# Placing the high and low parts of streamed weights: one place in a 256-byte line for all, or two for each product

## The chip, the cores and the metric

The kernel runs on one core of a Trainium2 chip. The metric is the device time of one launch in microseconds; the median of three runs of the kernel before is 1408.38 us (1407.89 to 1414.13). All rows shown come from one profiled execution.

## What is computed

The reference is one layer of a hybrid decoder on 256 tokens of width 2048, all in float32: a root-mean-square norm, an input projection, sliding-window attention beside a state-space mixer (whose inputs first go through a causal convolution along the tokens), an output projection, and then a feed-forward network with a convolution, a gate and a down projection. Cut to the lines that matter here:

```python
proj = xn @ w_in                                  # 2048 -> q, k, v, z, conv channels, dt
xbc = jax.nn.silu(_causal_dwconv(xbc, ssd_conv_w, ssd_conv_b))
...
h = h + jnp.concatenate([attn, y], axis=-1) @ w_out
...
u = _causal_dwconv(hn @ w_up, ffn_conv_w, ffn_conv_b)       # 2048 -> 2 * 5632
gate, val = u[..., :D_FF], u[..., D_FF:]
h = h + (jax.nn.silu(gate) * val) @ w_down                  # 5632 -> 2048
return _rmsnorm(h, norm_final)
```

## The kernel before, in words

Weights stream from HBM in blocks of 1 MB (tile `raw`, 128 partitions x 2048 floats). Each half block of 1024 floats per partition is split into a high part, rounded to the matmul's float32r type by ScalarE (`hi`, line 80), and a low part, the rest, subtracted by VectorE (`lo`, line 81). The activations are split in the same way and stay in memory, the high and the low row of a 128-row tile side by side: `xT` before the mixer, `h2T` before the feed-forward network. A product in this split form is high x high + high x low + low x high.

There are two kinds of product. `gemm_tok` keeps the activations stationary in TensorE's array and streams the weights past them, 512 columns at a time; query, key, value, gate, output and down projections go this way. `gemm_chan` keeps the weights stationary, 128 x 128 at a time, and streams the 256 tokens past them. It is used for two stages:

- The conv stage: 8 products of 512 output channels (two for each of four turns `zi`, with `gemm_tok` products between them). With `wide=False` each weight tile pair costs three matmuls of 256 columns: high weights on high tokens (line 229), high weights on low tokens (line 230), low weights on high tokens (line 231). That is 192 matmuls in a product and 1,536 in the stage.
- The up stage: 22 products of 512 output channels, one after the other (11 turns `c`, two products each). Each weight tile pair costs two matmuls: high weights on high and low tokens together, 512 columns (line 237), and low weights on the high tokens, 256 columns (line 235). That is 64 pairs in a product and 1,408 in the stage.

Every one of these matmuls is preceded by its own weight load (PEld in the profile), which runs beside the matmul before it: beside a 512-column matmul the low weights are loaded, beside a 256-column matmul of the up stage the next high weights.

`hi` and `lo` are rings of four tiles each, every tile beginning at a multiple of `LINE` = 256 bytes. A product's data begin `at` bytes into the tile. All slices used as weights begin a multiple of 512 bytes further on, and the token rows are 1024 bytes apart, so within one stage all weight tiles of a kind have one place modulo 256, and so have all token rows. Before the change the places are: `W_AT` = 0 for high and low weights of the up stage and of all `gemm_tok` products, `C_AT` = 64 for high and low weights of the conv stage; `X_AT` = 0 for `xT` and the other activations, `H_AT` = 32 for `h2T`. The order of the instructions comes from a scheduler that is run when the program is built.

Of the kernel before, what the change touches and what calls it, by code (L numbers as in the profile page):

```python
# [11 lines left out]
F32R = mybir.dt.float32r  # L12
# [7 lines left out]
P = 128  # L20
# [18 lines left out]
HALF = 1024  # L39
LINE = 256  # L40

W_AT, C_AT, X_AT, H_AT = 0, 64, 0, 32

PAR_MIX, PAR_ATT, PAR_SSD, PAR_FFN = 0, 16, 32, 48
PAR_CW, PAR_CB = 64, 192
# [7 lines left out]
def hymba(ctx, tc, x, xt, w_kd, w_in, w_out, w_up, w_down, par, vecs, gfin, con, out):  # L53
# [4 lines left out]
    wp = ctx.enter_context(tc.tile_pool(name="wp", bufs=1))  # L58
# [4 lines left out]
    def acc(tag="acc"):  # L63
        return ps.tile([P, 512], F32, tag=tag, name=tag, bufs=4)
# [9 lines left out]

    def split(raw, o, n, at):
        hi, lo = (
            wp.tile([P, HALF + C_AT // 4], F32R, tag=t, name=t, bufs=4, align_bytes=LINE)[:, at // 4 : at // 4 + n]
            for t in ("hi", "lo")
        )
        A.copy(out=hi, in_=raw[:, o : o + n])  # L80
        V.tensor_tensor(out=lo, in0=raw[:, o : o + n], in1=hi.bitcast(F32), op=ALU.subtract)  # L81
        return hi, lo

    def pieces(src, width, parts, load=None, work=None, at=W_AT):

        n = width // parts
        per = RAWW // n
        raws = [wp.tile([P, RAWW], F32, tag="raw", name="raw", bufs=3) for _ in range(-(-parts // per))]
        part = lambda h: raws[h // per][:, h % per * n : (h % per + 1) * n]
        if load:  # L90
            for h in range(parts):
                load(h)
                SY.dma_start(out=part(h), in_=src[:, h * n : (h + 1) * n])
        else:
            SY.dma_start(out=raws[0][:, :width], in_=src)
        out = []
        for h in range(parts):
            if work:
                work(h)
            out.append(split(part(h), 0, n, at))  # L100
        return out

    def acts(pool, at, **kw):
        return placed(pool, NKT * 2 * S, at, **kw).rearrange("p (k i s) -> p k i s", i=2, s=S)

    xT = acts(cp, X_AT, tag="xT", name="xT")
# [74 lines left out]
    def step(n=1):  # L181
        turn[0] += n
        while side and side[0][0] <= turn[0]:
            heappop(side)[2]()
# [24 lines left out]
                if i < nb - 1 or m < 3:  # L209
                    step()  # L210

    def gemm_chan(blocks, actT, evac, tag="acc", wide=True):

        b = [acc(tag) for _ in range(4)]
        nb = len(blocks)
        for i, src in enumerate(blocks):
            got = pieces(src, 2048, 2, at=W_AT if wide else C_AT)
            last = i == nb - 1
            for ks in [(0, 1, 2, 3)] if last else [(0, 1), (2, 3)]:
                for ct in range(4):  # L220
                    for k in ks:
                        hi, lo = got[k // 2]
                        kt = 4 * i + k
                        o = (k % 2) * 512 + ct * P
                        end = kt == NKT - 1
                        rh = actT[:, kt, 0, :]
                        wh, wl = hi[:, o : o + P], lo[:, o : o + P]
                        if not wide:
                            PE.matmul(out=b[ct][:, :S], lhsT=wh, rhs=rh, start=kt == 0, stop=False)  # L229
                            PE.matmul(out=b[ct][:, :S], lhsT=wh, rhs=actT[:, kt, 1, :], start=False, stop=False)  # L230
                            PE.matmul(out=b[ct][:, :S], lhsT=wl, rhs=rh, start=False, stop=end)  # L231
                            continue
                        for lo_turn in (True, False) if end else (False, True):
                            if lo_turn:
                                PE.matmul(out=b[ct][:, :S], lhsT=wl, rhs=rh, start=False, stop=False)  # L235
                            else:
                                PE.matmul(out=b[ct], lhsT=wh, rhs=actT[:, kt, :, :], start=kt == 0, stop=end)  # L237
                    if last:
                        evac(ct, b[ct])
                    if (ct < 3) if last else (ct % 2):  # L240
                        step()

    def conv(dst, b, rB, wcol, bias, taps, wide):

        u = up.tile([P, S], F32, tag="cu", name="cu", bufs=3)
        if wide:
            A.copy(out=u, in_=b[:, S:])
            V.tensor_tensor(out=u, in0=b[:, :S], in1=u, op=ALU.add)
            V.tensor_tensor(out=u, in0=u, in1=rB, op=ALU.mult)
        else:  # L250
            V.tensor_tensor(out=u, in0=b[:, :S], in1=rB, op=ALU.mult)
        A.activation(out=dst, in_=u, func=AF.Identity, scale=wcol(taps - 1), bias=bias)
        for j in range(1, taps):
            V.scalar_tensor_tensor(  # L254
                out=dst[:, j:], in0=u[:, : S - j], scalar=wcol(taps - 1 - j), in1=dst[:, j:],
                op0=ALU.mult, op1=ALU.add,
            )
# [336 lines left out]
    def decay_load(g):  # L594
        e = sp.tile([P, NT, HPG, P], F32, tag="e", name="e", bufs=2)
        G.dma_start(
            out=e.rearrange("p t h l -> p t (h l)"), in_=acs_d[:, g, :].partition_broadcast(P)
        )
        return e
# [162 lines left out]
    for zi in range(4):  # L762
        es, parts, zt = {}, {}, {}

        def z_load(zi=zi, zt=zt):
            zt[0] = sp.tile([P, NT, 512], F32, tag="zs", name="zs", bufs=1)
            G.dma_start(out=zt[0].rearrange("p t d -> p (t d)"), in_=z_d[zi])

        def decay_loads(zi=zi, es=es):
            for g in (2 * zi, 2 * zi + 1):  # L770
                es[g] = decay_load(g)

        for g in (2 * zi, 2 * zi + 1):
            u = up.tile([P, 4, S], F32, tag="u", name="u", bufs=2)

            def evac_u(ct, b, u=u, g=g, zt=zt):
                cidx = 2 * g + ct if ct < 2 else (16 + g if ct == 2 else 24 + g)
                conv(u[:, ct, :], b, r1B, lambda k: col(PAR_CW + 32 * k, cidx), col(PAR_CB, cidx), 4, False)
                A.activation(out=u[:, ct, :], in_=u[:, ct, :], func=AF.Silu)
                if g % 2 and ct == 3:  # L780
                    A.activation(out=zt[0], in_=zt[0], func=AF.Silu)

            def part(i, g=g, u=u, es=es, parts=parts):
                if i == 0:
                    parts[g] = ssd(g, es, u)
                parts[g][i]()

            gemm_chan([w_in[5 + 3 * zi + g % 2, i] for i in range(4)], xT, evac_u, wide=False)
            if g % 2 == 0:
                later((1 if zi else 11, decay_loads), (4 if zi else 14, z_load))  # L790
            later(*(
                (off, f) for off, f in zip(
                    (5, 7, 11, 13) if g % 2 else (4, 6, 10, 12) if zi else (13, 14, 18, 20),
                    (
                        lambda g=g, es=es: decay(g, es[g]), lambda part=part: part(0),
                        lambda part=part: part(1), lambda part=part: part(2),
                    ),
                )
            ))

        def gates(zi=zi, parts=parts, zt=zt):
            for g in (2 * zi, 2 * zi + 1):
                parts[g][3](zt[0])

        gemm_att(zi)
        later(
            (1, gates), (7, lambda zi=zi, parts=parts: parts[2 * zi][4]()),
            (9, lambda zi=zi, parts=parts: parts[2 * zi + 1][4]()), *(((10, open_hp),) if zi == 3 else ()),
        )
# [30 lines left out]
    for c in range(11):  # L840
        gate = up.tile([P, 4, S], F32, tag="u", name="gate", bufs=2)

        def evac_f(ct, b, val, c=c, gate=gate):
            i = 4 * c + ct
            ci = i + (NFT if val else 0)
            if val:
                dst = fp.tile([P, S], F32, tag="cv", name="cv", bufs=3)
            else:
                dst = gate[:, ct, :]
            conv(dst, b, r2B, lambda k: col(PAR_FW + 88 * k, ci), col(PAR_FB, ci), 3, True)  # L850
            if val:
                G.tensor_tensor(out=gT[:, i, :], in0=gate[:, ct, :], in1=dst, op=ALU.mult)  # L852
            else:
                A.activation(out=dst, in_=dst, func=AF.Silu)

        for val in range(2):
            gemm_chan(
                [w_up[2 * c + val, i] for i in range(4)], h2T, lambda ct, b, val=val: evac_f(ct, b, val),
                tag="aux" if val else "acc",
            )  # L860

    oacc = [[acc("acc" if t == 0 else "aux") for _ in range(4)] for t in range(NT)]
# [162 lines left out]
```

## Time and profile before

| | |
|---|---|
| median of three runs | 1408.38 us |
| the profiled execution | 1410.48 us |
| its span, first to last instruction | 1408.8 us |
| TensorE busy | 1388.7 us, 99% of the span |
| conv stage, first to last of its 8 products | about 270 to 553 us, with other products between |
| up stage | about 670 to 1160 us |
| down projection | about 1160 to 1390 us |

The span is what the trace covers; the 1.7 us between it and the time of that execution lie outside the program's instructions. A matmul's listed duration is longer than the distance from its start to the next start, since matmuls are pipelined; the distances between starts are what adds up.

### The profile page before, as it was taken

Reading aid. Unit: us, or ns where it says so; the run is one execution under the profiler, and the core shown is the slowest. Engines: PE = TensorE matmul, PEld = TensorE weight load, DVE = VectorE, ACT = ScalarE, POOL = GpSimd, SP = SyncE. Lnnn points to the kernel's source line nnn. Section 1 sums busy time; section 2 is a strip of 40 time slices with the busy share of each in tenths; the row PEclk is TensorE's granted clock in tenths of the full one; section 3 lists DMA queues with packets and bytes.
Section 4 is the critical chain, followed back from the end, with each engine's and each line's share of the span. In section 5 each row is a group of like instructions: output and inputs, shape, how many; then the busy total and the mean of one; then the engine's idle time right before and its main releaser. Section 6 shows DMA issues by size and latency. Waiting matters only on the chain.

```text
span 1408.8 us, 20546 instructions
## 1 busy us (share of the span) xinstructions
PE 1388.7 (99%) x7925; PEld 1219.9 (87%) x7925; DVE 969.4 (69%) x1448; ACT 785.4 (56%) x1245; POOL 173.8 (12%) x155
## 2 busy tenths in 40 slices
PE   8999999999999999999999999999999999999997
PEld 8788888997999999888888888888888888888886
DVE  5676876777777767655677768777786766555555
ACT  6666666656756555454555555555554554444444
POOL 0002112022121121200011001110011101000001
PEclk9999999999999999999999999999999999999999
DMA  8754444555656564565655555555555555555552
GB/s 293 271 181 154 176 150 165 184 183 177 235 194 211 193 235 161 207 222 184 221 190 181 178 209 183 198 188 180 202 186 185 195 189 187 201 184 204 183 205 90
DMA packets 44593, 271.76 MB, mean 193 GB/s; under 512 B 5056, under 2 KB 7232, under 8 KB 14672
## 3 DMA queue, kind: packets, MB, share of 16 engines
q1 hardware_dynamic: 40288, 254.69, 50.8%
q0 software_dynamic: 4208, 15.76, 3.6%
q8 instruction: 62, 1.02, 0.3%
q14 instruction: 35, 0.29, 0.1%
HBM read 264.11 MB, written 6.32 MB: 192 GB/s over the span
## 4 chain that ended last, share of the span: by engine, by line
PE 92%; DMA 3%; DVE 2%; ACT 1%; issue 1%; POOL 0%; SPq 0%; DVEq 0%; POOLq 0%; ACTq 0%
PE acc L237 11%; PE aux L237 11%; PE acc L170 11%; PE acc L168 11%; PE acc L169 11%; PE aux L235 6%; PE acc L235 6%; PE acc L231 4%; PE acc L229 4%; PE acc L230 4%; PE aux L169 3%; PE aux L170 3%; PE aux L168 3%; PE aux L464 1%; PE aux L673 1%
## 5 line engine op out<-in xcount | busy, mean ns | idle before, releaser
L81 DVE TENSOR_TENSOR lo<-raw,hi 128x1024 fp32r<-128x1024 f32 (+1 forms) x480 | 588.1, 1232 | 348.0 <-ACT hi L80 345.9
L80 ACT CAST hi<-raw 128x1024 fp32r<-128x1024 f32 (+1 forms) x480 | 492.1, 1034 | 416.8 <-PE aux L170 126.4
L237 PE MATMUL acc<-h2T,hi 128*128 128x512 f32 x704 | 243.4, 391 | 0.0
L237 PE MATMUL aux<-h2T,hi 128*128 128x512 f32 x704 | 243.0, 391 | 0.0
L235 PE MATMUL aux<-h2T,lo 128*128 128x256 f32 x704 | 191.1, 282 | 0.0
L235 PE MATMUL acc<-h2T,lo 128*128 128x256 f32 x704 | 191.0, 282 | 0.0
L237 PEld LDWEIGHTS aux<-h2T,hi 128*128 128x128 f32 x704 | 129.8, 188 | 24.6
L237 PEld LDWEIGHTS acc<-h2T,hi 128*128 128x128 f32 x704 | 129.8, 188 | 24.5
L229 PE MATMUL acc<-xT,hi 128*128 128x256 f32 x512 | 143.2, 282 | 0.0
L230 PE MATMUL acc<-xT,hi 128*128 128x256 f32 x512 | 143.1, 281 | 0.0
L231 PE MATMUL acc<-xT,lo 128*128 128x256 f32 x512 | 141.5, 279 | 0.7 <-DVE lo L81 0.7
L235 PEld LDWEIGHTS acc<-h2T,lo 128*128 128x128 f32 x704 | 132.9, 189 | 3.9
L235 PEld LDWEIGHTS aux<-h2T,lo 128*128 128x128 f32 x704 | 132.9, 189 | 3.8
L168 PE MATMUL acc<-hi,xT 128*128 128x512 f32 (+2 forms) x320 | 115.0, 378 | 5.4 <-ACT hi L80 5.4
L170 PE MATMUL acc<-hi,xT 128*128 128x512 f32 (+2 forms) x320 | 119.1, 374 | 0.0
L169 PE MATMUL acc<-lo,xT 128*128 128x512 f32 (+2 forms) x320 | 118.6, 373 | 0.0
L852 POOL TENSOR_TENSOR gT<-gate,cv 128x256 f32<-128x256 f32 x44 | 61.2, 1392 | 434.5 <-DVE cv L254 424.0
L231 PEld LDWEIGHTS acc<-xT,lo 128*128 128x128 f32 x512 | 96.1, 189 | 1.0 <-DVE lo L81 0.9
L230 PEld LDWEIGHTS acc<-xT,hi 128*128 128x128 f32 x512 | 96.5, 189 | 0.4
L229 PEld LDWEIGHTS acc<-xT,hi 128*128 128x128 f32 x512 | 95.9, 188 | 0.3
L168 PEld LDWEIGHTS acc<-hi,xT 128*128 128x128 f32 x320 | 59.6, 192 | 14.5 <-ACT hi L80 5.4
L170 PEld LDWEIGHTS acc<-hi,xT 128*128 128x128 f32 x320 | 61.2, 191 | 9.5
(221 smaller groups left out, 2288.5 us busy)
## 6 DMA issues: line engine op xcount, KB each, us to landing
raw<-in_w_up SPq DMA_DIRECT2D x88, 1024.0 KB, 4.8
raw<-in_w_in SPq DMA_DIRECT2D x68, 1024.0 KB, 4.9
raw<-in_w_down SPq DMA_DIRECT2D x44, 1024.0 KB, 4.8
raw<-in_w_out SPq DMA_DIRECT2D x32, 1024.0 KB, 4.8
raw<-in_w_kd SPq DMA_DIRECT2D x16, 272.0 KB, 4.8
e<-acs_d POOLq DMA_DIRECT2D x8, 512.0 KB, 6.6
xraw<-in_xt SPq DMA_DIRECT2D x16, 128.0 KB, 4.5
x_r<-in_x SPq DMA_DIRECT2D x2, 1024.0 KB, 7.2
```

The lines of the kernel that those rows point to most:

```text
L80: A.copy(out=hi, in_=raw[:, o : o + n])
L81: V.tensor_tensor(out=lo, in0=raw[:, o : o + n], in1=hi.bitcast(F32), op=ALU.subtract)
L168: PE.matmul(out=o, lhsT=lh, rhs=rh, start=first, stop=False)
L169: PE.matmul(out=o, lhsT=lh, rhs=rl, start=False, stop=False)
L170: PE.matmul(out=o, lhsT=ll, rhs=rh, start=False, stop=last)
L229: PE.matmul(out=b[ct][:, :S], lhsT=wh, rhs=rh, start=kt == 0, stop=False)
L230: PE.matmul(out=b[ct][:, :S], lhsT=wh, rhs=actT[:, kt, 1, :], start=False, stop=False)
L231: PE.matmul(out=b[ct][:, :S], lhsT=wl, rhs=rh, start=False, stop=end)
L235: PE.matmul(out=b[ct][:, :S], lhsT=wl, rhs=rh, start=False, stop=False)
L237: PE.matmul(out=b[ct], lhsT=wh, rhs=actT[:, kt, :, :], start=kt == 0, stop=end)
L464: PE.matmul(out=b[:, i * nk : (i + 1) * nk], lhsT=qs[:, jj, g0 + i, n * P : (n + 1) * P], rhs=ks[:, jj, part, 0:nk], start=part == 0, stop ...
L852: G.tensor_tensor(out=gT[:, i, :], in0=gate[:, ct, :], in1=dst, op=ALU.mult)
```

## The change

`split` takes two places instead of one, the first for `hi` and the second for `lo`. `gemm_chan` gets them from its caller: each of the 8 conv products has its own pair (`CONV_AT`) and each of the 22 up products has its own (`UP_AT`). The first sixteen up pairs have the high part at 0, 16, 32, ... 240 bytes and the low part at those sixteen values in another order; the last six are written out. The seventeenth, (0, 0), is the place before the change. `W_AT` becomes (0, 0), so all `gemm_tok` products keep their place. The tiles grow from 4160 to 4352 bytes; since each begins at a multiple of 256, they stood 4352 bytes apart already, and nothing else in memory moves. On each of the five engines the instructions and their order are the same as before.

```diff
-W_AT, C_AT, X_AT, H_AT = 0, 64, 0, 32
+
+W_AT, X_AT, H_AT = (0, 0), 0, 32
+CONV_AT = ((64, 0), (64, 192), (64, 32), (64, 96), (32, 64), (96, 64), (48, 80), (80, 48))
+UP_AT = tuple((16 * i, 16 * ((7 * i + 4) % 16)) for i in range(16)) + (
+    (0, 0), (0, 32), (32, 0), (96, 32), (32, 96), (0, 96)
+)
...
     def split(raw, o, n, at):
         hi, lo = (
-            wp.tile([P, HALF + C_AT // 4], F32R, tag=t, name=t, bufs=4, align_bytes=LINE)[:, at // 4 : at // 4 + n]
-            for t in ("hi", "lo")
+            wp.tile([P, HALF + LINE // 4], F32R, tag=t, name=t, bufs=4, align_bytes=LINE)[:, a // 4 : a // 4 + n]
+            for t, a in zip(("hi", "lo"), at)
         )
...
-    def gemm_chan(blocks, actT, evac, tag="acc", wide=True):
+    def gemm_chan(blocks, actT, evac, at, tag="acc", wide=True):
...
-            got = pieces(src, 2048, 2, at=W_AT if wide else C_AT)
+            got = pieces(src, 2048, 2, at=at)
...
-            gemm_chan([w_in[5 + 3 * zi + g % 2, i] for i in range(4)], xT, evac_u, wide=False)
+            gemm_chan([w_in[5 + 3 * zi + g % 2, i] for i in range(4)], xT, evac_u, CONV_AT[g], wide=False)
...
-                tag="aux" if val else "acc",
+                UP_AT[2 * c + val], tag="aux" if val else "acc",
```

## Rows read from the trace of the kernel before

**Rows 1.** The page: span, busy time, and the chain that ended last by engine.
```profile
span 1408.8 us, 20546 instructions
...
PE 1388.7 (99%) x7925; PEld 1219.9 (87%) x7925; DVE 969.4 (69%) x1448; ACT 785.4 (56%) x1245; POOL 173.8 (12%) x155
...
PE 92%; DMA 3%; DVE 2%; ACT 1%; issue 1%; POOL 0%; SPq 0%; DVEq 0%; POOLq 0%; ACTq 0%
```

**Rows 2.** The waits of TensorE over the whole span: total us, times, longest.
```profile
PE acc L168 <- ACT hi L80: 5.4, 1, 5.4
PE acc L168 <- DVE cu L251: 1.4, 1, 1.4
...
PE acc L231 <- DVE lo L81: 0.7, 1, 0.7
```

**Rows 3.** Windows: second up product, the twenty after it; last columns clock, DMA share, GB/s.
```profile
693.40:715.60 22.20, 22.20 (x129) 19.64 (x128) 15.70 (x26) 12.83 (x21) 0.00 (x0) 1.00 0.53 189
715.60:1160.15 444.55, 444.55 (x2562) 392.91 (x2560) 330.88 (x486) 246.58 (x365) 56.47 (x40) 1.00 0.54 190
```

**Rows 4.** Timeline of TensorE, up stage: start, duration, instruction; 44 pairs between first and last.
```profile
716.31 0.39 PE L237 MATMUL acc<-h2T,hi 128*128 128x512 f32 x1
716.54 0.28 PE L235 MATMUL acc<-h2T,lo 128*128 128x256 f32 x1
716.66 0.39 PE L237 MATMUL acc<-h2T,hi 128*128 128x512 f32 x1
...
731.57 0.39 PE L237 MATMUL acc<-h2T,hi 128*128 128x512 f32 x1
```

**Rows 5.** Timeline of TensorE, down projection: 101 matmuls from first to last.
```profile
1200.05 0.39 PE L170 MATMUL aux<-hi,gs 128*128 128x512 f32 x1
...
1222.95 0.39 PE L169 MATMUL acc<-lo,gs 128*128 128x512 f32 x1
```

**Rows 6.** Timeline of TensorE, conv stage: 78 matmuls from first to last.
```profile
430.09 0.28 PE L231 MATMUL acc<-xT,lo 128*128 128x256 f32 x1
...
439.28 0.28 PE L231 MATMUL acc<-xT,lo 128*128 128x256 f32 x1
```

**Rows 7.** The same product later: 150 matmuls from first to last.
```profile
443.66 0.28 PE L229 MATMUL acc<-xT,hi 128*128 128x256 f32 x1
...
460.66 0.28 PE L229 MATMUL acc<-xT,hi 128*128 128x256 f32 x1
```

**Rows 8.** Timeline, output projection: 40 matmuls, four transposes, nine from 589.17 to 591.26.
```profile
579.21 0.39 PE L169 MATMUL acc<-lo,yT 128*128 128x512 f32 x1
...
588.27 0.39 PE L170 MATMUL acc<-hi,yT 128*128 128x512 f32 x1
588.51 0.60 PE L159 MATMUL aux<-con_t,y 128*128 128x128 f32 x4
588.86 0.48 PE L168 MATMUL acc<-hi,yT 128*128 128x512 f32 x1
589.17 0.40 PE L169 MATMUL acc<-lo,yT 128*128 128x512 f32 x1
589.41 0.40 PE L170 MATMUL acc<-hi,yT 128*128 128x512 f32 x1
...
591.26 0.39 PE L169 MATMUL acc<-lo,yT 128*128 128x512 f32 x1
```

**Rows 9.** Splits in the conv stage, 428 to 479 us: count, busy us, mean ns, idle before.
```profile
L81 DVE TENSOR_TENSOR lo<-raw,hi 128x1024 fp32r<-128x1024 f32 x16 | 19.6, 1228 | 8.0 <-ACT hi L80 8.0
L80 ACT CAST hi<-raw 128x1024 fp32r<-128x1024 f32 x16 | 16.6, 1050 | 10.0 <-PE acc L230 6.1 <-PE acc L170 2.3 <-issue 1.6
```

**Rows 10.** The same in the up stage, 760 to 1140 us.
```profile
L81 DVE TENSOR_TENSOR lo<-raw,hi 128x1024 fp32r<-128x1024 f32 x137 | 170.7, 1256 | 90.0 <-ACT hi L80 90.0
L80 ACT CAST hi<-raw 128x1024 fp32r<-128x1024 f32 x138 | 142.6, 1047 | 130.0 <-PE acc L237 75.8 <-PE aux L237 54.2
```

## The prediction

> **What bounds the kernel now.** I read the page first. TensorE is busy for 99% of the span and makes up 92% of the chain that ended last [rows 1]. The waits of TensorE come next: the longest is 5.4 us, at the kernel's start, and the list is soon at 0.7 us [rows 2]. So nothing feeds TensorE too late; the kernel lasts as long as its matmuls need. Then the windows: the second up product takes 22.2 us and the twenty after it 444.55 us, 22.23 us each, with a granted clock of 1.00 (2.4 GHz), VectorE busy for 74% of that time (330.88 of 444.55), ScalarE for 55% and the DMA engines for 54% [rows 3]. Any time won or lost per matmul in that stage goes straight into the end.
>
> Last, the distances between matmul starts, since the change can act on nothing else. They are what the reader is to see:
>
> - A 512-column matmul that has settled takes 226.7 ns in the down projection (22.90 us over 101) [rows 5].
> - A 256-column matmul of the conv stage takes 113.3 ns in one stretch (17.00 us over 150) [rows 7] and 117.8 ns in another stretch of the same product (9.19 us over 78) [rows 6]. Instructions, shapes and places are the same in both; what differs is how the stream stands in time after the last interruption.
> - An up pair, 512 and 256 columns, takes 346.8 ns (15.26 us over 44); the single steps are 230 and 120 ns at the timeline's resolution [rows 4]. The two undisturbed steps together would be 226.7 + 113.3 = 340.0 ns. So the up pair pays 6.8 ns, about as much as the slow conv step loses, 4.5 ns, and a little on the long matmul.
> - In the output projection 40 matmuls take 226.5 ns each (9.06 us); after four transposes have broken the stream, the next nine take 232.2 ns each (2.09 us), single steps up to 240 ns [rows 8].
>
> I read this as two streams, weight loads and token reads, that sometimes get in each other's way, by a few ns per matmul, and mostly fall into a rhythm that is repeated until something interrupts it. Which rhythm is to be had may depend on the places; that is what the change touches. That places have any part in it no row shows, since each stage has only one pair of places.
>
> **The change part by part.** Nothing is added, removed or reordered on any engine; the number of matmuls, weight loads, splits and DMAs stays, and no wait is new. What is left are three terms, each the same instruction at another byte.
>
> *Up pairs.* 21 of 22 products get new places (the seventeenth keeps its own): 21 x 64 = 1,344 pairs. No row shows a pair at another place, so I bound it. Below: 340.0 ns, both steps undisturbed [rows 5, 7], -6.8 ns a pair, -9.1 us. Above: the largest single long step with the slow short one, 240 + 117.8 = 357.8 ns [rows 6, 8], +11.0 ns a pair, +14.8 us. Between them lies the pair that never settles: the mean of the broken stretch with the slow short step, 232.2 + 117.8 = 350.0 ns, +3.2 ns a pair, +4.3 us. I take this one. The new places are spread over the whole line, high and low independently, and the nearest thing in the trace to an arbitrary position of two streams against each other is the stretch after a break, before a rhythm is found.
>
> *Conv matmuls.* All 8 products get a new place for at least one part: 1,536 matmuls. All slow against all fast is 1,536 x 4.45 ns = 6.8 us [rows 6, 7]. Long stretches of both are there now, so I leave half of it in each direction, -3.4 to +3.4 us, and take 0: a mixture before, a mixture after.
>
> *Splits.* ScalarE and VectorE write to other bytes. At 64 in the conv stage they take 1050 and 1228 ns [rows 9], at 0 in the up stage 1047 and 1256 ns [rows 10], so the place moves them by 2% at most, and not in one direction. For the 16-byte places no row exists. From below I see no reason for a gain that counts, since nobody waits for them. From above: VectorE idles for 113.7 us of the 444.55 us [rows 3], in which 160 splits are made, so each could grow by 0.7 us, more than half of itself, before VectorE bounds the stage. I take 0. What covers them is TensorE's own work; without that cover the 2% would be 25 ns x 240 splits of the two stages, 6 us.
>
> Sum: 1410.48 + 4.3 = 1414.8 us for the profiled execution. The median lies 2.1 us below that execution, so against 1408.38 the forecast is 1412.7 us, +0.3%.
>
> **A rule weighed against the rows.** The same product runs at 113.3 and at 117.8 ns a matmul [rows 6, 7], at one and the same pair of places. The Trainium skill (TensorE: Matmul & The Clock Gate, Step-by-step: what each phase is for) says that TensorE reads weights and moving data through two independent ports, so that loading the next weights takes no read bandwidth from the running matmul. By that rule no place could matter and the sum would be 0. The rows show that something costs 4.5 ns, but not that it is the place.
>
> **The rivals.**
>
> *Places do not matter.* The change then does nothing. For it: two speeds at one place [rows 6, 7], and after a break the stream of the output projection returns to full speed by itself [rows 8]. Against it: the up stage repeats 22.23 us for twenty products and pays 6.8 ns in every pair [rows 3, 4], while the down projection, with other places, pays nothing [rows 5]; but their shapes differ too. Time: 1408.4 us, 1406 to 1411 with chance rhythms in the conv stage.
>
> *Faster: parted places leave both loads undisturbed.* The load of the high weights runs beside the short matmul, that of the low weights beside the long one; with a place for each, both could fit, which one shared place may not allow. For it: 340.0 ns is reached in parts elsewhere. Against it: the places go all around the line, so it would have to hold at almost every one. Every product free gives 1408.4 - 9.1 - 3.4 = 1395.9 us; half of them, 1402 us.
>
> *Slower by more: at many places the streams collide for good.* Then the broken stretch of the output projection is not a passing state but the rhythm itself, and the short matmul waits for its weight load beyond 117.8 ns. It decides from 7.0 us on: 7.0 us / 1,344 = 5.2 ns a pair, a mean pair of 352 ns. At the upper bounds it gives 1408.4 + 14.8 + 3.4 = 1426.6 us. For it: single steps of 240 ns exist [rows 8], and nothing covers them [rows 2]. Against it: no stretch that lasts is worse than 117.8 ns for 256 columns.
>
> **How the numbers follow.** About 0.5%, 7 us, is what a measurement of this kernel can tell from no change: 1401.3 to 1415.4 us is the same. The forecast, a small loss within that, gets 0.40, with a range of its own from 1407 to 1415 us. That places do not matter gets 0.15. Faster gets 0.17, of which 0.08 lies beyond 0.5%. Slower by more gets 0.28, since its threshold is only 2 ns a pair above my forecast. So: faster 0.08, same 0.40 + 0.15 + 0.09 = 0.64, slower 0.28. The range from 1402 to 1421 us leaves out the lower half of the faster case and the upper third of the slower one, less than 2 in 10 together.
>
> **What would show it right or wrong.** The up stage of the changed kernel is 22 products behind each other, each readable by itself. The seventeenth, at (0, 0), must again take 22.2 us; if it does not, the time depends on something besides the places. If the forecast holds, the others scatter between 21.8 us (64 x 340.0 ns, and the product's edges) and 22.9 us (64 x 357.8 ns), with a mean near 22.4 us, and the conv stage shows both speeds again. If all stay at 22.2 us, places do not matter. If the mean is below 22.0 or above 22.6 us, one of the other two cases has come. The splits should stay near 1050 and 1230 ns and TensorE's list of waits as short as it is. The prediction is wrong if a place costs far more than the rows know of, or if the products that stand at good places outnumber the others.

## The result, and the profile after

| | before | after |
|---|---|---|
| median | 1408.83 us (8 runs) | 1417.64 us (8 runs) |
| profiled execution, its span | 1410.48, 1408.8 us | 1417.63, 1415.9 us |
| conv stage, its 8 products added, each from its first matmul to its last | 200.4 us | 203.9 us |
| up stage, first matmul to the end | 490.4 us | 493.6 us |

The ratio is 1.0054 with an interval from 1.0040 to 1.0067: 5.6 to 9.4 us slower. The two profiles differ by 7.1 us: 0.6 us before the conv stage begins, 3.4 us from there to the start of the up stage, 3.2 us in the up stage, nothing behind it. The medians differ by more, 8.8 us, since the profiled execution of the kernel before was 1.6 us longer than the median of its runs.

The page of the changed kernel, the lines that answer to [rows 1], and the two groups of splits from its fifth part:

```profile
span 1415.9 us, 20546 instructions
...
PE 1395.7 (99%) x7925; PEld 1222.2 (86%) x7925; DVE 973.1 (69%) x1448; ACT 785.8 (55%) x1245; POOL 170.0 (12%) x155
...
PE 92%; DMA 3%; DVE 2%; issue 1%; ACT 1%; SPq 0%; POOL 0%; DVEq 0%; POOLq 0%; ACTq 0%
...
L86 DVE TENSOR_TENSOR lo<-raw,hi 128x1024 fp32r<-128x1024 f32 (+1 forms) x480 | 591.5, 1239 | 350.7 <-ACT hi L85 349.4
L85 ACT CAST hi<-raw 128x1024 fp32r<-128x1024 f32 (+1 forms) x480 | 492.2, 1034 | 423.2 <-PE aux L175 128.8
```

The waits of TensorE in the changed kernel, which answer to [rows 2]:

```profile
PE acc L173 <- ACT hi L85: 5.4, 1, 5.4
PE aux L146 <- DVE diag L145: 2.1, 1, 2.1
PE acc L173 <- DVE cu L256: 1.2, 1, 1.2
```

The wait on `diag` is not new; it stood at 1.2 us before. The 0.7 us wait of the conv stage has shrunk to 0.4 us. As many instructions, TensorE busy 7.0 us longer at the same share of the span, no new wait, splits within 1% of what they were: the loss is in the matmuls themselves. The timeline of TensorE in the changed kernel (start, duration, instruction; lines are five further on) shows it. Shown are three stretches of the conv stage, the third and the seventeenth and eighteenth up product by their first matmuls, and inside the third a piece of its rhythm:

```profile
307.31 0.28 PE L235 MATMUL acc<-xT,hi 128*128 128x256 f32 x1
...
317.17 0.28 PE L235 MATMUL acc<-xT,hi 128*128 128x256 f32 x1
...
355.32 0.28 PE L234 MATMUL acc<-xT,hi 128*128 128x256 f32 x1
...
365.10 0.28 PE L236 MATMUL acc<-xT,lo 128*128 128x256 f32 x1
...
369.09 0.28 PE L235 MATMUL acc<-xT,hi 128*128 128x256 f32 x1
...
378.93 0.28 PE L236 MATMUL acc<-xT,lo 128*128 128x256 f32 x1
...
383.45 0.28 PE L235 MATMUL acc<-xT,hi 128*128 128x256 f32 x1
...
719.89 0.39 PE L242 MATMUL acc<-h2T,hi 128*128 128x512 f32 x1
...
724.12 0.40 PE L242 MATMUL acc<-h2T,hi 128*128 128x512 f32 x1
724.35 0.28 PE L240 MATMUL acc<-h2T,lo 128*128 128x256 f32 x1
724.47 0.40 PE L242 MATMUL acc<-h2T,hi 128*128 128x512 f32 x1
724.70 0.28 PE L240 MATMUL acc<-h2T,lo 128*128 128x256 f32 x1
724.82 0.40 PE L242 MATMUL acc<-h2T,hi 128*128 128x512 f32 x1
725.06 0.28 PE L240 MATMUL acc<-h2T,lo 128*128 128x256 f32 x1
725.18 0.40 PE L242 MATMUL acc<-h2T,hi 128*128 128x512 f32 x1
...
742.49 0.39 PE L242 MATMUL aux<-h2T,hi 128*128 128x512 f32 x1
...
1033.46 0.40 PE L242 MATMUL acc<-h2T,hi 128*128 128x512 f32 x1
...
1055.68 0.40 PE L242 MATMUL aux<-h2T,hi 128*128 128x512 f32 x1
...
1077.87 0.39 PE L242 MATMUL acc<-h2T,hi 128*128 128x512 f32 x1
```

In the up stage the third product, at (32, 32), takes 742.49 - 719.89 = 22.60 us; its pairs come in threes of 1.06 us, 353 ns a pair against the 346.8 ns of [rows 4]. The seventeenth, left at (0, 0), takes 22.22 us as before, and the eighteenth, at (0, 32), 22.19 us. In the conv stage the product at (64, 192) runs 87 matmuls in 9.86 us, 113.3 ns each, the speed of [rows 7]. From the product at (64, 32) into the next, at (64, 96), 120 matmuls take 14.36 us, 119.7 ns each, more than the slow stretch of [rows 6]. The part at (64, 32) takes 120.0 ns each (9.84 us over 82), while an earlier stretch of that same product takes 117.8 ns (9.78 us over 83): one place can still have two paces.

### The profile page after: what moved, and what is told of

It reads as the page before. It is cut to its first block, busy times and chain, and to the rows that moved or that the text cites. A ratio compares the mean times of both kernels' runs of the same rounds, so it can differ in the third digit from the quotient of the medians.

```text
span 1415.9 us, 20546 instructions
## 1 busy us (share of the span) xinstructions
PE 1395.7 (99%) x7925; PEld 1222.2 (86%) x7925; DVE 973.1 (69%) x1448; ACT 785.8 (55%) x1245; POOL 170.0 (12%) x155
## 4 chain that ended last, share of the span: by engine, by line
PE 92%; DMA 3%; DVE 2%; issue 1%; ACT 1%; SPq 0%; POOL 0%; DVEq 0%; POOLq 0%; ACTq 0%
PE acc L242 12%; PE aux L242 11%; PE acc L175 11%; PE acc L174 11%; PE acc L173 11%; PE acc L240 6%; PE aux L240 6%; PE acc L234 4%; PE acc L235 4%; PE acc L236 4%; PE aux L174 3%; PE aux L175 3%; PE aux L173 3%; PE aux L469 1%; DMA raw<-in_w_in 1%
## 5 line engine op out<-in xcount | busy, mean ns | idle before, releaser
L86 DVE TENSOR_TENSOR lo<-raw,hi 128x1024 fp32r<-128x1024 f32 (+1 forms) x480 | 591.5, 1239 | 350.7 <-ACT hi L85 349.4
L85 ACT CAST hi<-raw 128x1024 fp32r<-128x1024 f32 (+1 forms) x480 | 492.2, 1034 | 423.2 <-PE aux L175 128.8
L175 PE MATMUL acc<-hi,xT 128*128 128x512 f32 (+2 forms) x320 | 118.9, 374 | 0.0
L857 POOL TENSOR_TENSOR gT<-gate,cv 128x256 f32<-128x256 f32 x44 | 61.7, 1402 | 437.3 <-DVE cv L259 425.8
```

Of the source, the lines that this page charges most:

```text
L175: PE.matmul(out=o, lhsT=ll, rhs=rh, start=False, stop=last)
```

## The experiments

Up stage and up product times below are distances between first matmuls in the profiles; a conv product's time goes from its first matmul to its last, and a matmul that reaches the next in about 113 ns is called fast. They tell more than the whole span: the conv stage begins between 266.8 and 272.4 us in the profiles of this study, whatever the change, and that start alone moves a span by some us. Two theories stood at the outset. **Place**: a product's pace belongs to the places of its weights and tokens. **Rhythm by chance**: a product falls into one pace or another by how its stream happens to begin, as the conv matmuls of [rows 6, 7] do at one place. ([Rows 7] begin in the product of [rows 6] and run over into the next, which starts at 452.84 us; the pair of places is the same in both.)

### Each half of the change alone

The up places alone, with conv back at (64, 64):

```diff
-CONV_AT = ((64, 0), (64, 192), (64, 32), (64, 96), (32, 64), (96, 64), (48, 80), (80, 48))
+CONV_AT = ((64, 64),) * 8
```

> Only the 22 up products get their new places, the conv products stand at (64, 64) as before. If a pair's time belongs to the places of its product, the conv stage is that of before, each up product takes what it took in the changed kernel (22.2 to 22.6 us, the longest at (144, 48), (32, 32) and (128, 192)), and the span is 1408.8 + 3.2 = 1412.0 us. If the rhythm that a product falls into depends on when it begins, the up products' times come out in another pattern, since the stage starts some 4 us earlier.

Measured: ratio 1.0022 (1.0012 to 1.0031), about +3.1 us; up stage 493.57 us, the same to 0.01 us as in the changed kernel, conv stage 199.9 us. Every up product has the time that it had there to 0.01 us, though the stage began 3.1 us earlier.

The conv places alone, with all up products at (0, 0):

```diff
-UP_AT = tuple((16 * i, 16 * ((7 * i + 4) % 16)) for i in range(16)) + (
-    (0, 0), (0, 32), (32, 0), (96, 32), (32, 96), (0, 96)
-)
+UP_AT = ((0, 0),) * 22
```

> Only the 8 conv products get their new places, all up products stand at (0, 0). If places add up, the up products take 22.2 us each again, the conv stage loses 3.9 us, and the span is 1412.7 us. If the loss of the conv stage came from chance rhythms after its interruptions, it differs by some us from that of the changed kernel.

Measured: ratio 1.0028 (1.0017 to 1.0039), about +3.9 us; up stage 490.37 us, that of before; conv stage 203.95 us, against 203.89 in the changed kernel. (The profiled span of 1409.9 us is short because the conv stage began at 268.0 us.) The two halves add up within their intervals: 0.22% and 0.28% for 0.54%.

### The places moved to other products

```diff
+CONV_AT = CONV_AT[2:] + CONV_AT[:2]
+UP_AT = UP_AT[11:] + UP_AT[:11]
```

> The changed kernel with its lists of places rotated, 11 on in the up stage and 2 on in the conv stage, so that each pair of places stands in another product. If time belongs to the place, the long up products wander along: (32, 32) takes 22.6 us and (0, 32) 22.2 us where they now stand, the one conv product that gained, (64, 192), gains as product 7, and the span stays at 1416 us. If time belongs to the product and its neighbours, the list of times by product stays as in the changed kernel.

The timeline of TensorE in this run, by the first matmuls of the products that now hold (0, 32) and (32, 32), each with the first of the product behind it:

```profile
805.94 0.40 PE L244 MATMUL acc<-h2T,hi 128*128 128x512 f32 x1
...
828.13 0.39 PE L244 MATMUL aux<-h2T,hi 128*128 128x512 f32 x1
...
962.51 0.39 PE L244 MATMUL aux<-h2T,hi 128*128 128x512 f32 x1
...
985.12 0.39 PE L244 MATMUL acc<-h2T,hi 128*128 128x512 f32 x1
```

(0, 32) takes 22.19 us as the seventh product as it did as the eighteenth, (32, 32) takes 22.61 us as the fourteenth as it did as the third. All 20 places that stand behind another up product in both kernels keep their times to 0.02 us. In the conv stage (64, 192) is again the one product with 156 of 192 matmuls at 113 ns. The span is 1413.1 us rather than 1416, with a conv stage that began 2.1 us earlier. Place holds, chance falls for the up stage. Each of the 20 also changes from the `acc` result tiles to the `aux` ones or back, so which of them a product writes is not what counts.

### All conv products at the one place that gained

```diff
-CONV_AT = ((64, 0), (64, 192), (64, 32), (64, 96), (32, 64), (96, 64), (48, 80), (80, 48))
+CONV_AT = ((64, 192),) * 8
```

The up products stand at (0, 0) here.

> All conv products at (64, 192), the only place of the eight that gained (25.08 us against 25.72 us), all up products at (0, 0). If the place decides, each conv product runs most of its matmuls at 113 ns and the stage gains about 0.6 us a product, 8 x 0.6 = 5 us: span 1404 us. If the gain was chance, the span is that of before, 1408.8 us, within 2 us.

The timeline of TensorE, conv stage, 148 matmuls from the first to the last row:

```profile
369.57 0.28 PE L235 MATMUL acc<-xT,hi 128*128 128x256 f32 x1
...
386.34 0.28 PE L236 MATMUL acc<-xT,lo 128*128 128x256 f32 x1
```

That is 113.3 ns a matmul in the very stretch that took 119.7 ns in the changed kernel, and 132 to 170 of the 192 matmuls of every product take 113 ns. Yet the stage gains only 1.4 us (198.97 us against 200.39) and the ratio is 0.9994 (0.9985 to 1.0003). How many matmuls are fast goes with the place, but my 0.6 us a product was read from one that in the kernel before was held up for 0.7 us by a wait (the last of [rows 2]) and had only 75 fast matmuls. In the run with the up places alone the same product, at (64, 64) again but without that wait, takes 25.07 us, as long as the 25.08 us that I had credited to (64, 192). The others had 100 to 117 fast matmuls of 192 already, and some 50 more at 4.45 ns are 0.2 us. The sum of the stage is itself loose: over the six profiles with conv at (64, 64) it goes from 199.8 to 200.4 us. The fourth, sixth and eighth product are steadier: 25.62 or 25.63 us at (64, 64) in all six, 25.45 to 25.47 us in all four at (64, 192), some 0.17 us a product.

### A quarter of the DMAs and splits

```diff
-            got = pieces(src, 2048, 2, at=at)
+            got = got if wide and i else pieces(src, 2048, 2, at=at)
```

> The up places of the changed kernel, conv at (64, 64). Each up product loads and splits only the first of its four blocks and uses it four times, so it computes something else, with a quarter of the weight DMAs and splits. If the pair's time is a matter between TensorE's own two reads, weight loads and tokens, each product keeps its time to 0.05 us: 22.40 at (16, 176), 22.61 at (32, 32), 22.19 at (0, 32). If DMA writes or the splits of ScalarE and VectorE get in its way, products come down towards 64 x 340.0 ns = 21.8 us.

The windows of the product at (32, 32), in the changed kernel and then in this run (us, then busy time and count of PE, PEld, DVE, ACT, POOL, then clock, DMA share, GB/s):

```profile
719.89:742.49 22.60, 22.60 (x129) 19.62 (x128) 18.58 (x30) 12.75 (x21) 5.83 (x4) 1.00 0.54 190
```
```profile
717.91:740.52 22.61, 22.61 (x130) 19.62 (x128) 11.61 (x23) 6.96 (x15) 3.58 (x4) 1.00 0.15 47
```

The DMA share falls from 0.54 to 0.15, ScalarE from 12.75 to 6.96 us, and the product lasts as long as before. All 22 keep their times to 0.01 us (sum 493.57 us again). So it is a matter of TensorE's own reads, or of what lies behind them, not of the amount of traffic that fills memory.

### Long and short matmuls by themselves

Both runs use the first block four times as above, so they compute something else too; they have the sixteen 16-byte places, high and low alike, in the first sixteen products, and 4, 8, 12, 36, 40 and 104 bytes in the last six. Both read high weights alone. The first leaves out the matmuls of the low weights:

```diff
-                            if lo_turn:
-                                PE.matmul(out=b[ct][:, :S], lhsT=wl, rhs=rh, start=False, stop=False)
-                            else:
+                            if not lo_turn:
                                 PE.matmul(out=b[ct], lhsT=wh, rhs=actT[:, kt, :, :], start=kt == 0, stop=end)
```

> The up stage without the matmuls of the low weights (256 columns), with blocks used four times as in the run with few streams: 64 matmuls of 512 columns in a product, high weights at each of the sixteen 16-byte places, and at 4, 8, 12, 36, 40 and 104 bytes. If a weight load fits beside a long matmul at any place once a rhythm is found, all products settle at 226.7 ns a matmul, 14.5 us. If the place counts there too, some settle at 230 to 236 ns.

The timeline of TensorE, long matmuls alone: the products at 32 and at 96 by their first matmuls, each with the first of the next:

```profile
698.60 0.39 PE L238 MATMUL acc<-h2T,hi 128*128 128x512 f32 x1
...
713.11 0.39 PE L238 MATMUL aux<-h2T,hi 128*128 128x512 f32 x1
...
757.48 0.39 PE L238 MATMUL acc<-h2T,hi 128*128 128x512 f32 x1
...
772.40 0.39 PE L238 MATMUL aux<-h2T,hi 128*128 128x512 f32 x1
```

14.51 us at 32, 14.92 us at 96, for 64 matmuls each: 226.7 and 233.1 ns. Settled at 226.7 ns are the places 16, 32 and 48 alone, the tokens' own place (32) and its two 16-byte neighbours. Nearness is not enough: at 36 and 40 bytes, between 32 and 48, the products take 14.87 and 14.77 us, 232 and 231 ns a matmul. Of the other 16-byte places, 64 to 192 take 232 to 234 ns and 208 to 240 take 229 to 232 ns (the first product, at 0, waits for its data and is left out here and below). So the place of the weights, which the load alone reads, counts beside a long matmul too.

The second keeps one short matmul for each weight tile. The long and the short matmul of the pair both go, and the steps behind a product use the first 256 columns of its result alone:

```diff
-                                PE.matmul(out=b[ct][:, :S], lhsT=wl, rhs=rh, start=False, stop=False)
...
-                                PE.matmul(out=b[ct], lhsT=wh, rhs=actT[:, kt, :, :], start=kt == 0, stop=end)
+                        PE.matmul(out=b[ct][:, :S], lhsT=wh, rhs=rh, start=kt == 0, stop=end)
```

> The up stage with one matmul of 256 columns for each weight tile, high weights on high tokens only, blocks used four times, at the same 22 places. Here a weight load has to fit beside each short matmul. If the place of the weights against the tokens decides, some places settle at 113.3 ns and others at 117.8 ns or more, and the list is not flat. If the short matmul is simply too short, all settle at one time above 113.3 ns.

The timeline of TensorE, short matmuls alone, again the products at 32 and at 96:

```profile
682.34 0.28 PE L236 MATMUL acc<-h2T,hi 128*128 128x256 f32 x1
...
690.01 0.28 PE L236 MATMUL aux<-h2T,hi 128*128 128x256 f32 x1
...
712.70 0.28 PE L236 MATMUL acc<-h2T,hi 128*128 128x256 f32 x1
...
719.96 0.28 PE L236 MATMUL aux<-h2T,hi 128*128 128x256 f32 x1
```

7.67 us at 32 and 7.26 us at 96: 120 ns and 113.4 ns a matmul. The place 96, 64 bytes behind the tokens, is the only one of these places that settles at 113.3 ns, from its third matmul on; the other 16-byte places settle at 116.7 to 120.1 ns, the six other places at 115.6 to 120.0 ns. Long and short matmuls want different places.

### More places, and the tokens moved too

The scan of 22 other pairs:

```diff
+UP_AT = (
+    (208, 0), (208, 64), (208, 128), (208, 192), (208, 224), (240, 240), (240, 0), (240, 64), (240, 128), (240, 176),
+    (224, 224), (224, 0), (224, 160), (80, 80), (80, 16), (80, 176), (80, 240), (64, 64), (64, 128), (64, 192),
+    (144, 144), (0, 192),
+)
```

> 22 other pairs of places in the up stage and 8 in the conv stage. If the pair of 346.7 ns is the least that this alternation of 512 and 256 columns allows, no product falls below 22.18 us, and some lie up to 22.7 us as in the changed kernel. If a place exists at which both steps are undisturbed, it shows a pair of 340.0 ns and a product of 21.8 us. In the conv stage a place is good when most of its steps take 113 ns, as at (64, 192); at random places I expect 117 to 119 ns.

Measured: up products from 22.21 us, at (80, 80) and (224, 160), to 22.60 us, at (224, 224), the first product aside; the least pair is 346.7 ns again. In the conv stage (192, 64) has 117 fast matmuls of 192, as (64, 64) mostly had, the other seven new places 1 to 51; the stage takes 203.0 us.

Then the up places and the tokens moved by the same 16 bytes:

```diff
-W_AT, X_AT, H_AT = (0, 0), 0, 32
+W_AT, X_AT, H_AT = (0, 0), 0, 48
...
+UP_AT = tuple(((h + 16) % LINE, (l + 16) % LINE) for h, l in UP_AT)
```

> The up places of the changed kernel all moved 16 bytes on (modulo 256), and the tokens too, from 32 to 48; conv at (64, 64). If only the distance between weights and tokens counts, every up product keeps its time to 0.02 us: 22.40 at the second, 22.61 at the third, 22.64 at the tenth, 22.23 at the seventeenth, and the sum stays 493.6 us. If places count by themselves, the list is another.

The timeline of TensorE in this run: the seventh product, at (112, 240), with its first steps and, settled, 42 pairs between the two rows in its middle, and the first matmul of the eighth:

```profile
803.83 0.40 PE L243 MATMUL acc<-h2T,hi 128*128 128x512 f32 x1
804.07 0.28 PE L241 MATMUL acc<-h2T,lo 128*128 128x256 f32 x1
...
807.93 0.39 PE L243 MATMUL acc<-h2T,hi 128*128 128x512 f32 x1
...
822.22 0.39 PE L243 MATMUL acc<-h2T,hi 128*128 128x512 f32 x1
...
825.64 0.39 PE L243 MATMUL aux<-h2T,hi 128*128 128x512 f32 x1
```

The list is another one. At (96, 224) with tokens at 32 the product took 22.51 us; 16 bytes on it takes 825.64 - 803.83 = 21.81 us, and its settled pair is 14.29 us / 42 = 340.2 ns, both steps undisturbed: the lower bound of the prediction, which none of the 43 pairs of places measured with tokens at 32, without a wait, had reached. (32, 192) takes 21.89 us, (240, 112) 21.95 us; (32, 32) with tokens at 32 had taken 22.61, and its counterpart (48, 48) takes 22.28. The distance between weights and tokens is thus not all that counts. Against the run with the up places alone nothing else changed its place in memory. No run moved the tokens alone.

### Matmuls of one length in groups of eight

For these two the up stage's order is changed: per half block all long matmuls, then all short ones, in the last block four and four.

```diff
+                if wide:
+                    todo = [(ct, k, part) for part in (3, 4) for ct, k in turns]
+                    if last:
+                        todo = [(ct, k, part) for ct in range(4) for part in (4, 3) for k in ks]
...
+                    elif part == 3:
+                        PE.matmul(out=b[ct], lhsT=wh, rhs=actT[:, kt, :, :], start=kt == 0, stop=end)
+                    else:
+                        PE.matmul(out=b[ct][:, :S], lhsT=wl, rhs=rh, start=False, stop=False)
...
+CONV_AT = ((64, 192),) * 8
+UP_AT = ((32, 96),) * 22
```

> The up stage in another order: per half block first the eight matmuls of high weights (512 columns), then the eight of low weights (256 columns), in the last block four and four. High weights at the tokens' place (32), where long matmuls alone settled at 226.7 ns, low weights 64 on (96), where short ones alone settled at 113.3 ns; conv at (64, 192). If those distances are what counts and a run of eight is long enough to settle, an up product takes 64 x 340.0 ns = 21.8 to 21.95 us, the stage 6 to 9 us less, and with the conv stage's 1.4 us the kernel takes 1399 to 1402 us. If each change of length breaks the rhythm, products stay at 22.2 us or more.

The timeline of TensorE in this run, where rows of one line are merged; the sixth product begins with the first row, the seventh with the last:

```profile
781.97 1.98 PE L244 MATMUL aux<-h2T,hi 128*128 128x512 f32 x8
783.78 1.11 PE L246 MATMUL aux<-h2T,lo 128*128 128x256 f32 x8
784.73 2.00 PE L244 MATMUL aux<-h2T,hi 128*128 128x512 f32 x8
786.56 1.11 PE L246 MATMUL aux<-h2T,lo 128*128 128x256 f32 x8
...
804.23 0.39 PE L244 MATMUL acc<-h2T,hi 128*128 128x512 f32 x1
```

The first eight long matmuls take 1.81 us, the second eight 1.83 us, 227 and 229 ns each; the short ones 0.95 us a group, about 118 ns, and not 113. A product takes 22.26 us, the kernel's ratio is 1.0002 (0.9993 to 1.0011). For the long matmuls a run of eight is too short: by their single starts the first five of a group behind short ones take 228 to 236 ns and only the last three 225 to 227 ns. For the short ones that is not shown. They take 117 to 119 ns from the first on and stay there in the one run of twelve in each product, where alone at 96 they were at 113 ns from the third on. Their weights come from the `lo` tiles here and came from the `hi` tiles there; no run tells this apart from the change of length.

The same with `UP_AT = ((96, 32),) * 22`:

> The same order with the two places swapped, high weights at 96 and low weights at 32. Alone, long matmuls settled at 233.3 ns and short ones at 120.0 ns there: 353.3 ns a pair, 22.6 us a product, 0.8 us more than with the places the right way round. If the order makes the gain and not the places, it is as fast as the other.

Measured: 22.45 us a product, 0.19 us more than with the places the other way round, not 0.8. The long matmuls take 233.3 ns, as alone; the short ones 117.7 ns, not the 120.0 ns at which they settle alone. The places count. The 117.7 ns are a mean: by single starts the short matmuls go from 112 to 121 ns in one group and reach 120 ns after two steps in the next, so they settle in part.

### The best places measured, order as before

`UP_AT = ((240, 208),) * 22`, `CONV_AT = ((64, 192),) * 8`, tokens at 32.

> Places alone, order as before: all up products at (240, 208), the shortest product measured (22.18 us), all conv products at (64, 192). By the sums of the profiles the up stage gains 22 x 0.05 = 1.0 us and the conv stage 1.4 us: 2.4 us, 0.17%, under what a comparison can tell from no change. If the places of single products do not carry over to a stage that has them all, up products differ from 22.18 us.

Measured: ratio 0.9986 (0.9976 to 0.9996), about 2.0 us faster than before; conv stage 198.8 us (-1.6), up stage 489.5 us (-0.9), up products of 22.19 us from the second on. It beats both kernels, by little; its interval just leaves out no change.

## Why the prediction was right, and where it was not

The time lies inside the range (1402 to 1421 us), 4.9 us above the forecast of 1412.7 us and just beyond the 0.5% that I had set as the border of "the same"; the case of a larger loss had been given 0.28. The measured interval, 0.40 to 0.67%, lies on both sides of that border. That the sum came so near is in part luck: the up term was forecast 1.1 us too large and the conv term 3.5 us too small.

- **What bounds the kernel**: right. No wait came or went that counts, and what the matmuls lost, 3.2 us in the up stage and 3.5 us in the conv stage, is all but 0.4 us of the 7.1 us between the profiles.
- **The term of the up pairs**, +4.3 us from 350.0 ns a pair: 3.2 us was measured, 3.2 / 1,344 = 2.4 ns a pair rather than 3.2. Of the 20 moved products behind the first, which waits, eight stayed within 0.05 us of the old 22.23 us; the other twelve took 22.34 to 22.64 us. The stretch after a break turned out a fair stand-in for an arbitrary place, but by luck and not for the reason that I gave: a product at a bad place does settle, into a repeated rhythm of one to four pairs (eight at (16, 176)) that is as slow as an unsettled stream, like the 1.06 us for three pairs above.
- **The term of the conv matmuls**, 0 within -3.4 to +3.4 us: this step failed. The stage lost 3.5 us by its products' durations. "A mixture before, a mixture after" did not hold: at seven of the eight new pairs 2 to 26 of 192 matmuls are fast, where (64, 64) has 75 to 117. And the upper bound was no bound, since "all slow" was priced at 117.8 ns: in the changed kernel the slow matmuls of the stage take 118.9 ns in the mean, at (64, 32) 120.0 ns in a long stretch. As the kernel before shows the largest of six sums at (64, 64), 199.8 to 200.4 us, the loss may be put at 3.5 to 4.1 us. That the old place was an unusually good one no row could show; one place per stage says nothing of how the others lie.
- **Splits**: right, 1239 and 1034 ns in the mean against 1232 and 1034 before, on the two pages.
- **Places do not matter**: fell. The same place gives the same product time to 0.02 us in another position, with another start, and with a quarter of the streams. What [rows 6, 7] show is that some places have two rhythms, as (64, 32) has in the changed kernel. By the rule of the Trainium skill that the prediction weighed (TensorE: Matmul & The Clock Gate, Step-by-step: what each phase is for) loading weights would cost the running matmul nothing. The runs do not agree: short matmuls alone take 113.4 against 120 ns at two places of the weights with the same tokens, and the weights' place is read by the load alone. What in the load costs this, no run shows.
- **Faster by parted places**: fell for tokens at 32, where none of 43 pairs of places settled clearly below 346.7 ns a pair; it is true of single products with tokens at 48.
- **Slower by more**: it gave a slow pace that lasts as the rhythm itself, and that is what the slow products show, though not that a collision makes it; the mean pair of 352 ns at which it was to decide alone was not reached (349.2 ns), and the conv stage made up the rest.

What stays open is the law behind the places, and whether it is the weight load that meets the token reads or something else within TensorE: no run took the loads away. Distance alone does not give it, and what long and short matmuls cost alone does not add up: by themselves long matmuls at 32 and short ones at 96, both with high weights, cost nothing; alternating, with 32 for the high and 96 for the low weights, they take 346.7 ns a pair and 22.26 us a product. Not run, too, is the version that the last finding points to: all up products at (112, 240) with the tokens at 48, and conv at (64, 192). From the profiles' sums it would gain 22 x (22.23 - 21.81) = 9.2 us and 1.4 us, an estimate of about 1398 us.

## What to carry to other kernels

Where a stream of matmuls is bound by TensorE alone, look at the distance between starts and not at busy time, and ask whether its steps equal the best that any stretch of the kernel shows; a few ns at a thousand matmuls are what is left to gain. If places in memory can shift it, give every product its own place and read the profile product by product: one run is a table of 22 places, each exact to 0.02 us, while the times of whole runs scatter by several us (1407.83 to 1414.13 us for the kernel before). A place found good for one alternation of lengths is good for that alternation only; measure it again in the order in which it will stand, and move the moving operand as well as the weights.

## What the runs showed of the hardware that was not expected

- The time of a matmul in float32r depends on the byte places of the weights and the tokens: 113.3 to 120.1 ns for 256 columns, 226.7 to 234.4 ns for 512, at the granted clock of 1.00 and without any wait.
- A product runs in a rhythm that repeats exactly: one pair of 346.7 ns at (0, 0), three pairs in 1.06 us at (32, 32). DMA traffic between 47 and 190 GB/s does not shift it. Taken from the single starts, every settled cycle of the 63 up products behind the first, in the changed kernel, the scan and the run with the tokens moved, is a whole multiple of 6.67 ns to 0.2 ns: pairs of 340.0, 346.7 or 353.3 ns are 51, 52 or 53 of them, the three pairs at (32, 32) 159. Matmuls alone settle in the same steps, 113.3 and 120.0 ns being 17 and 18, 226.7 and 233.3 ns 34 and 35. Means in between, such as 350.0 ns a pair, come from cycles of several pairs.
- Moving both operands by 16 bytes turned a product of 22.51 us into one of 21.81 us and another of 22.26 us, at (64, 0), into one of 22.60 us.
